# Attention's second pass of scores on 64 rows, two parts of the keys side by side

## The chip, the cores and the metric

The kernel runs on one core of one Trainium2 chip. The metric is the time of the program on the device, in microseconds (us); the page and the views quoted below come from one execution recorded by the hardware profiler.

## The reference

One layer of a streaming encoder on 2048 frames of width 1024. A normalized input is projected to ten groups of columns; one branch is attention in chunks, the other a retention with decay; both are gated, projected, mixed, projected again, added to the input and normalized. The change is in the attention branch, in the first `einsum` of this function:

```python
CHUNK = 64; N_LEFT_CHUNKS = 8; A_HEADS = 8; A_HEAD_DIM = 64

def chunk_band_attention(q, k, v, rel_bias):
    """Each frame attends to its own chunk and the previous N_LEFT_CHUNKS chunks."""
    ...
    def one_sequence(args):
        ...
        s = jnp.einsum('nqhd,nkhd->nhqk', qc, k_band).astype(jnp.float32) * scale + bias[None]
        s = jnp.where(valid[:, None, None, :], s, NEG_INF)
        w = jax.nn.softmax(s, axis=-1).astype(vb.dtype)
        o = jnp.einsum('nhqk,nkhd->nqhd', w, v_band)
        return o.reshape(S, H, d)
```

All in float32, with 8 heads of 64 numbers each. A chunk of 64 queries sees 576 keys.

## The kernel before, in words

**Two parts for each number.** TensorE multiplies in a format (`F32R`) narrower than float32. So each operand is split into a high part, its rounded value, and a low part, what the rounding left. A product of two numbers is then high times high, plus high times low, plus low times high. For keys and queries of 64 numbers this fits the 128 rows of the array: a key tile `kt` holds the high parts of one head's keys on rows 0 to 63 and the low parts on rows 64 to 127, and a query tile `qa` holds both parts of the queries, each of them written twice, on rows 0 to 63 and again on rows 64 to 127. With the high queries as weights, one matmul over 128 rows gives high times high plus high times low: the first pass. With the low queries as weights, a second matmul over the same 128 rows gives low times high (and low times low, which counts for nothing): the second pass.

**Units and slots.** Attention runs in two stages: `heads(0)` for the blocks 0 and 1 of 512 frames, `heads(1)` for the blocks 2 and 3. In a stage, `units` lists (head, block) pairs, 16 of them. The function `slot` issues the work of one slot: for the unit m that is being finished, the transposes of weights and their products with the values (`weighted`), and for the unit after it the scores and the softmax (`soft`). A unit has 12 slots (9 for block 0); `plan` says in which slot which group is handled. In the second stage `soft` for the query tiles t = 0, 1, 2, 3 (128 queries each) of the next unit stands in the slots 2, 6, 8 and 10, in the first stage for block 1 in the slots 1, 3, 5 and 7 of the unit before.

**Fillers.** After each slot `fill(1.0)` runs one step of the dense projections (the gates: matmuls of 512 columns into `ps_g_...`), and `later(n, ...)` puts work on the other engines n steps on. The order on each engine is the order of issue, kept by `keep_in_program_order`; the transfers of attention are on SyncE's queue (SP), which issues them in that order, each one waiting for what it needs.

**`soft`.** For a block b > 0 a query tile sees 640 keys. The scores go to `wide`, three banks of PSUM; since a matmul writes into one bank, the 640 keys are cut into `parts`: 384 and 256 for even t, 256 and 384 for odd t. So a call issues four matmuls: the first pass of both parts, then the second pass of both parts. For block 0 there is one part of 128 to 512 keys and so two matmuls. After that VectorE adds the bias and takes the minimum (`least`), ScalarE takes the exponential, and GpSimd divides.

**Loads.** `load_k` brings a unit's keys, 1024 of them (the block before and the block itself), in slot 6, two units ahead, into one of two buffers. `load_q` brings the queries of two tiles. `load_u` brings the unit's gate into a buffer of the ring `E`, in slot 6; that ring has `E_ATT` = 11 buffers of 128 x 512 numbers and also holds the queries, the values, the transposed weights and the outputs. GpSimd multiplies the unit's output with the gate in `out_`, called by the last group of `weighted`, some five slots into the next unit, and `put` then sends the product off.

Of the kernel before, what the change touches and what calls it, by code (L numbers as in the profile page):

```python
# [11 lines left out]
F32 = mybir.dt.float32  # L12
F32R = mybir.dt.float32r
# [8 lines left out]
P = 128  # L22
# [6 lines left out]
B = 512  # L29
# [23 lines left out]
LO_LAG = 4  # L53
CS = 6
E_PROJ = 19
E_ATT = 11
E_RET = 22
E_MRG = 23
PR_BUFS = 5
# [14 lines left out]
def hybrid_kernel(  # L74
# [30 lines left out]
    def r32(ap):  # L105
        return ap.bitcast(F32)
# [7 lines left out]
    def E(name, dt=F32, shape=(P, 512)):  # L114
        return epool[0].tile(list(shape), dt, tag="e", name=name)
# [4 lines left out]
    def D(name, shape, dt=F32):  # L120
        return dram.tile(list(shape), dt, name=name)
# [31 lines left out]
    pe, act, dve, pool = Ordered(nc.tensor), Sometimes(nc.scalar), Sometimes(nc.vector), Sometimes(nc.gpsimd)  # L153
    dma = Ordered(nc.sync).dma_start
# [19 lines left out]
    kascr = [[D(f"kas_{h}_{b}", [P, B], F32R) for b in range(NB)] for h in range(HEADS)]  # L174
# [70 lines left out]
    def later(n, fn):  # L245

        order[0] += 1
        deferred.append((steps[0] + n, order[0], fn, free[0]))
        deferred.sort(key=lambda e: e[:2])
# [21 lines left out]
    class Chunk:  # L271
# [14 lines left out]
        def half(self, j, c):  # L286
            if self.job.paired[self.c]:

                return self.raw[j].rearrange("p k (i h c) -> p k h i c", i=4, h=2)[:, :, c]
            return self.raw[j][:, :, c * P:(c + 1) * P]  # L290
# [45 lines left out]
    class Strassen(Chunk):  # L336
        tag = ""
# [335 lines left out]
    def step():  # L673
        steps[0] += 1
        while deferred and deferred[0][0] <= steps[0]:
            emit()
        going = next(stream[0], None) is not None
        free[0] = False
        while deferred and not going:
            emit()  # L680
        return going

    def fill(n):
        credit[0] += n
        while credit[0] >= 1.0 and steps[0] < limit[0] and step():
            credit[0] -= 1.0
        credit[0] = min(credit[0], 1.0)
# [722 lines left out]
    def attention(s, sbp, ps_wide):  # L1410
# [3 lines left out]
        kts, vts, qts, bts, uts, oas, prs = {}, {}, {}, {}, {}, {}, {}  # L1414
        units = [(h, b) for h in range(HEADS) for b in (2 * s, 2 * s + 1)]
        wholes = {}

        def load_k(h, b):
            kts[h, b] = sbp.tile([P, 2 * B], F32R, tag="kt", bufs=2, name=f"ka_{h}_{b}")
            for n in range(1 if b == 0 else 0, 2):  # L1420
                dma(r32(kts[h, b][:, n * B:n * B + B]), r32(kascr[h][b - 1 + n]))

        def load_v(h, b):
            vts[h, b] = E(f"va_{h}_{b}", F32R, (P, 4, P))
            dma(r32(vts[h, b]).rearrange("p t c -> p (t c)"), r32(vascr[h][b]))

        def load_vs(h, b):
            if s and b == 2:
                load_v(h, 1)
            load_v(h, b)  # L1430

        def load_q(h, b, un):
            q = E(f"qa_{h}_{b}_{un}", F32R, (P, 2, T))
            rows = qascr[h // 2][b][64 * (h % 2):64 * (h % 2) + 64, un]
            for half in range(2):
                dma(r32(q[64 * half:64 * half + 64]), r32(rows))
            qts[h, b, un] = q

        def load_u(h, b):
            uts[h, b] = E(f"ua_{h}_{b}")[0:64]  # L1440
            dma(uts[h, b], uascr[h // 2][b][64 * (h % 2):64 * (h % 2) + 64])

        def load_bias(h):

            row = escr[h]
            bt = sbp.tile([P, WIN], F32, tag="bt", bufs=2, name=f"bt_{h}")
            if s:
                near = bt[:, 384:640]
                dma(near, bandscr[h])
            else:  # L1450
                near = E(f"near_{h}")[:, 0:256]
                dma(near, bass.AP(tensor=row.tensor, offset=row.offset, ap=[[1, P], [1, 256]]))
            bts[h] = bt, near

        def turn_bias(h):

            bt, near = bts[h]
            bts[h] = bt
            edge = near[:, 0:1] if s else near[:, 255:256]

            def far():
                for n in range(3):
                    act.copy(bt[:, P * n:P * n + P], edge.broadcast_to([P, P]))

            def close():
                if not s:
                    act.copy(bt[:, 384:640], near[:, ::-1])
                    pool.memset(bt[0:64, WIN - 64:WIN], MASK)
                    put(4, bandscr[h], bt[:, 384:640])
                pool.memset(bt[64:128, 0:64], MASK)  # L1470

            later(1, close)
            later(0, far)

        def soft(h, b, t):

            un, a = divmod(t, 2)
            nm = f"{h}_{b}_{t}"
            if b > 0:
                s0, c0 = ((P, 384), (WIN + P, 256))[a]  # L1480
                parts = [(0, c0), (c0, WIN)]
                w, k0 = WIN, t * P
            else:
                s0 = 1024 * a
                w, k0 = (t + 1) * P, B
                parts = [(0, w)]
            sp = wide[:, s0:s0 + w]
            k = kts[h, b]
            q = qts[h, b, un]
            for part in range(2):  # L1490
                for j0, j1 in parts:
                    pe.matmul(
                        sp[:, j0:j1], q[:, part, a * P:(a + 1) * P], k[:, k0 + j0:k0 + j1],
                        start=(part == 0), stop=(part == 1),
                    )
            mn = small.tile([P, 1], F32, tag="mn", name=f"mn_{nm}")
            rsum = small.tile([P, 1], F32, tag="rsum", name=f"rsum_{nm}")
            bt = bts[h]

            def least():  # L1500
                pair, at = (t, 0) if b > 0 else ((0, 0), (1, 0), (1, 2 * P), (0, P))[t]
                if (h, b, pair) not in wholes:
                    wholes[h, b, pair] = sbp.tile([P, WIN], F32, tag="pr", bufs=PR_BUFS, name=f"pr_{nm}")
                prs[h, b, t] = wholes[h, b, pair][:, at:at + w]
                dve.tensor_tensor_reduce(
                    prs[h, b, t], sp, bt[:, WIN - w:WIN], 1.0, 3.0e38, ALU.add, ALU.min, mn,
                )

            def exps():
                pr = prs[h, b, t]  # L1510
                act.activation(pr[:, 0:w], pr[:, 0:w], AF.Exp, bias=mn, scale=-1.0, accum_out=rsum)

            def normed():
                pr = prs[h, b, t]
                dve.reciprocal(rsum, rsum)
                pool.tensor_scalar(pr[:, 0:w], pr[:, 0:w], rsum, 1.0, ALU.mult, ALU.mult)

            later(1, least)
            later(2, exps)
            later(4, normed)  # L1520
# [53 lines left out]
        def slot(m, n, groups, softs):  # L1574

            after = units[m + 1] if m + 1 < len(units) else None
            if n == 0 and after:
                h, b = after
                load_q(h, b, 1)
                if b == 2 * s and h + 1 < HEADS:  # L1580
                    load_bias(h + 1)
                if b == 2 * s + 1 and h + 1 < HEADS:
                    turn_bias(h + 1)
            if n == 6:
                if m + 2 < len(units):
                    load_k(*units[m + 2])
                if m >= 0:
                    load_u(*units[m])
            if n in groups and m >= 0:
                weighted(*units[m], groups[n])  # L1590
            if n in softs and after:
                soft(*after, softs[n])

        load_bias(0)
        load_k(*units[0])
        load_q(*units[0], 0)
        fill(12)
        turn_bias(0)
        fill(2)
        for m in range(-1, len(units)):  # L1600
            length, *plans = plan(units[m][1] if m >= 0 else 2 * s + 1)
            for n in range(length):
                slot(m, n, *plans)
                if n == length - 2 and m + 2 < len(units):
                    load_q(*units[m + 2], 0)
                if n == length - 1 and m + 1 < len(units):
                    load_vs(*units[m + 1])
                fill(ATT_FILL if m >= 0 or n > 1 else 0)
        fill(PV_LAG + 3)

# [257 lines left out]
    for s in range(2):  # L1868
        jobs.append(Job(f"ba{s}", 4, w_stream(w_out_attn, [T * c for c in range(4)], 1), ep_ba(s),
                        kh=1, resident=RYA[s], before=before_ba(s)))  # L1870
# [59 lines left out]
    def heads(s):  # L1930

        st = open_phase(f"att{s}", E_ATT)
        with tc.tile_pool(name=f"sbp{s}", bufs=1, reuse_waits="tile") as sbp:
# [22 lines left out]
    for key in ("b11", "b12", "b21", "b22"):  # L1956
        ch.b[key] = E(f"{key}_p1", shape=(P, 4, P))
        j, h = int(key[1]) - 1, int(key[2]) - 1
# [83 lines left out]
```

## Time and profile before

| | us |
|---|---|
| median of 3 runs | 1908.64 (1907.68 to 1913.85) |
| the profiled execution | 1909.69 |
| its span, first to last instruction | 1907.9 |
| scores of the first stage, first matmul to last | 341.4 to 542.8 |
| scores of the second stage, first matmul to last | 1052.6 to 1296.3 |

How to read the rows that follow: an operation is written as output<-inputs by the names in the program, with partitions x elements. PE is TensorE's matmul, PEld its weight load, DVE VectorE, ACT ScalarE, POOL GpSimd, and SPq the queue of transfers that SyncE issues. `wide` are the scores, `tp` the transposes of the weights, `po` the products with the values, `ps_g_...` the dense filler. Every row has the same line number, since all instructions are issued by one helper; so the names tell them apart. A matmul's duration contains its way through the array; the next matmul starts before that is over, so the distance from start to start is what it costs in a stream. A row of a wait reads: engine and what it was about to do, what it waited for, us in total, times, longest.

### The profile page before, as it was taken

The page shows a single profiled execution, that of the slowest core. Times are in us where ns is not written, and L with a number is a line of the kernel's source. Part 1 is how long each engine was busy: PE and PEld are TensorE (multiplying, and loading weights), DVE is VectorE, ACT ScalarE, POOL GpSimd, SP SyncE. Part 2 cuts the span into 40 slices and gives each one's busy share as a digit, 9 for nine tenths or more (in the row PEclk, how much of TensorE's full clock was granted, in tenths as well). Part 3 has the DMA queues.
Part 4 walks back from the last instruction along what each step waited for, and adds up shares of the span by engine and source line. Part 5 has one row for each costly group of instructions (what it writes and reads, how often), then busy time and mean ns, then how long its engine had stood idle before and what let it go on. Part 6 is the DMA issues. An engine that isn't in the chain of part 4 may idle for free. (4 is left out here: it accounts for less than half of the span.)

```text
span 1907.9 us, 31062 instructions
## 1 busy us (share of the span) xinstructions
PE 1866.9 (98%) x10213; PEld 1604.4 (84%) x10213; DVE 1355.7 (71%) x2456; ACT 933.1 (49%) x1931; POOL 665.3 (35%) x583
## 2 busy tenths in 40 slices
PE   7999999999999999999999999999999999999998
PEld 6899889888888888899889888887888878888886
DVE  6879888677655658889798677765546766767665
ACT  7555554666654455443333666664455321223544
POOL 0102105455645561001105554554564000002775
PEclk9999999999999999999999999999999999999999
DMA  6586976666549987775776656555998999986673
GB/s 197 158 275 200 282 265 213 185 193 185 175 144 278 279 257 258 231 233 195 222 247 202 185 165 180 166 150 155 275 283 265 326 355 345 322 291 227 209 238 127
DMA packets 325553, 435.88 MB, mean 228 GB/s; under 512 B 29880, under 2 KB 191184, under 8 KB 325392
## 3 DMA queue, kind: packets, MB, share of 16 engines
q1 hardware_dynamic: 260096, 368.35, 60.7%
q10 hardware_dynamic: 65296, 65.55, 11.2%
q8 instruction: 81, 1.33, 0.3%
q14 instruction: 80, 0.66, 0.1%
HBM read 288.14 MB, written 145.64 MB: 227 GB/s over the span
## 5 line engine op out<-in xcount | busy, mean ns | idle before, releaser
L143 POOL TENSOR_SCALAR pr<-pr,rsum 128x640 f32<-128x640 f32 (+4 forms) x128 | 100.0, 781 | 197.7 <-DVE rsum L143 130.7
L143 DVE TENSOR_TENSOR ptl<-tp,pth 128x512 fp32r<-128x512 f32 (+1 forms) x168 | 100.3, 597 | 91.7 <-ACT pth L143 77.8
L143 ACT ACTIVATE pr<-pr,mn 128x640 f32<-128x640 f32 (+4 forms) x128 | 97.9, 765 | 123.3 <-DVE mn L143 97.3
L143 PE MATMUL ps_g_x<-r,wh_g 128*128 128x512 f32 x448 | 141.5, 397 | 1.0 <-ACT u_g L143 0.9
L143 PE MATMUL ps_g_z<-r,wh_g 128*128 128x512 f32 x448 | 141.1, 396 | 0.0
L143 POOL TENSOR_TENSOR l_vr<-vrt,h_vr 128x512 fp32r<-128x512 f32 x32 | 47.7, 1492 | 202.4 <-DMA qrs<-l_q 131.6
L143 POOL TENSOR_TENSOR t_out<-raw_out 128x512 f32<-128x512 f32 x7 | 14.1, 2008 | 263.2 <-DVE wl_out L143 263.2
L143 DVE CUSTOM_DVE_ANT_0 pr<-wide,bt 128x640 f32<-128x640 f32 (+4 forms) x128 | 93.7, 732 | 16.5 <-PE wide L143 13.5
L143 ACT CAST pth<-tp 128x512 fp32r<-128x512 f32 (+1 forms) x168 | 85.3, 507 | 38.9 <-PE tp L143 34.2
L143 PE MATMUL wide<-ka,qa 128*128 128x384 f32 (+1 forms) x448 | 94.9, 327 | 2.9 <-DVE mn L143 2.7
L143 DVE TENSOR_TENSOR sm<-sr,dm 128x384 f32<-128x384 f32 x64 | 35.6, 556 | 85.3 <-PE sr L143 33.9
L143 ACT CAST wh_p<-raw_p 128x512 fp32r<-128x512 f32 x111 | 67.9, 618 | 51.0 <-PE ps_p_y L143 18.2
L143 POOL TENSOR_TENSOR sl<-sm,sh 128x384 fp32r<-128x384 f32 x64 | 69.8, 1090 | 64.8 <-ACT sh L143 44.0
L143 PEld LDWEIGHTS tp<-ident,pr 128*128 128x128 f32 x560 | 71.8, 141 | 23.5 <-POOL pr L143 1.0
L143 PEld LDWEIGHTS ps_g_x<-r,wh_g 128*128 128x128 f32 x448 | 79.6, 189 | 13.9 <-ACT u_g L143 2.3
L143 PEld LDWEIGHTS ps_g_z<-r,wh_g 128*128 128x128 f32 x448 | 79.5, 188 | 12.4
L143 PE MATMUL tp<-ident,pr 128*128 128x128 f32 x560 | 89.0, 272 | 0.3
L143 PE MATMUL ps_g_z<-r,wl_g 128*128 128x512 f32 x224 | 88.2, 394 | 0.0
L143 PE MATMUL ps_g_x<-r,wl_g 128*128 128x512 f32 x224 | 88.1, 393 | 0.0
L143 POOL TENSOR_TENSOR wl_g<-t_g,wh_g 128x512 fp32r<-128x512 f32 x56 | 75.5, 1349 | 35.1 <-ACT wh_g L143 33.8
L143 DVE TENSOR_TENSOR wl_p<-raw_p,wh_p 128x512 fp32r<-128x512 f32 x111 | 79.5, 723 | 7.7 <-ACT wh_p L143 5.4
L143 POOL TENSOR_TENSOR t_g<-raw_g,t_g 128x512 f32<-128x512 f32 x56 | 73.8, 1318 | 28.1 <-issue 8.9
(927 smaller groups left out, 6016.7 us busy)
## 6 DMA issues: line engine op xcount, KB each, us to landing
raw_g<-in_w_in_dram ACTq DMA_DIRECT2D x56, 512.0 KB, 4.9
raw_p<-in_w_in_dram ACTq DMA_DIRECT2D x50, 512.0 KB, 5.8
qa<-qas SPq DMA_DIRECT2D x128, 128.0 KB, 3.4
qr<-qrs SPq DMA_DIRECT2D x128, 128.0 KB, 4.8
vr<-vrs SPq DMA_DIRECT2D x64, 256.0 KB, 5.6
ka<-kas SPq DMA_DIRECT2D x56, 256.0 KB, 4.1
va<-vas SPq DMA_DIRECT2D x40, 256.0 KB, 3.4
kds<-kdt_k SPq DMA_DIRECT2D x32, 256.0 KB, 4.8
```

The lines of the kernel that those rows point to most:

```text
L143: return tc.keep_in_program_order(op(*a, **k))
```

## The change

The second pass (low parts of the queries, row 1 of the query tile) is taken over 64 rows only: low queries times the high parts of the keys. One part of the keys is taken from `kt`, rows 0 to 63, as before; the other from a new tile `both`, on whose rows 64 to 127 a copy of the high parts of 512 of the unit's 1024 keys is loaded (`load_again`, two transfers for a unit). The queries' copy on rows 64 to 127 is the weight there. The shorter of the two matmuls is issued first. Where a tile's copy is not yet there (t = 0 of a unit in the second stage), and for block 0, the second pass takes rows 0 to 63 for all parts, one after the other. Rows 0 to 63 of `both` hold the unit's gate, which had a buffer in the ring `E`; the ring has one buffer fewer, and the gate is loaded in slot 7 and not 6.

```diff
-E_ATT = 11
+E_ATT = 10
...
+        both = sbp.tile([P, B], F32, tag="both", name="both")
...
+            if b == 1:
+                load_again(h, b)
+
+        def load_again(h, b):
+            dma(both[64:128, 0:P], r32(kascr[h][b - 1][0:64, 3 * P:]))
+            dma(both[64:128, P:], r32(kascr[h][b][0:64, 0:3 * P]))
...
         def load_u(h, b):
-            uts[h, b] = E(f"ua_{h}_{b}")[0:64]
+            uts[h, b] = both[0:64]
             dma(uts[h, b], uascr[h // 2][b][64 * (h % 2):64 * (h % 2) + 64])
...
-            for part in range(2):
+            qc = slice(a * P, (a + 1) * P)
+
+            def half(n, j0, j1):
+                kh = (both.bitcast(F32R)[64:128, k0 + j0 - 3 * P:k0 + j1 - 3 * P] if n else k[0:64, k0 + j0:k0 + j1])
+                pe.matmul(sp[:, j0:j1], q[64 * n:64 * n + 64, 1, qc], kh, start=False, stop=True)
+
+            for j0, j1 in parts:
+                pe.matmul(sp[:, j0:j1], q[:, 0, qc], k[:, k0 + j0:k0 + j1], start=True, stop=False)
+            if b > 0 and (t or not s):
+                for n, (j0, j1) in sorted(enumerate(parts if t < 3 else parts[::-1]), key=lambda x: x[1][1] - x[1][0]):
+                    half(n, j0, j1)
+            else:
                 for j0, j1 in parts:
-                    pe.matmul(
-                        sp[:, j0:j1], q[:, part, a * P:(a + 1) * P], k[:, k0 + j0:k0 + j1],
-                        start=(part == 0), stop=(part == 1),
-                    )
+                    half(0, j0, j1)
...
                 if m + 2 < len(units):
                     load_k(*units[m + 2])
-                if m >= 0:
-                    load_u(*units[m])
+            if n == 7 and m >= 0:
+                load_u(*units[m])
...
         load_k(*units[0])
+        if s:
+            load_again(*units[0])
...
                     load_vs(*units[m + 1])
+                    if s and m + 2 < len(units):
+                        load_again(*units[m + 2])
```

## The prediction

> **What bounds the kernel now.** I read the page first, then the windows of the two attention stages, then what TensorE waited for there, and last single instructions of one slot.
>
> ```profile
> span 1907.9 us, 31062 instructions
> PE 1866.9 (98%) x10213; PEld 1604.4 (84%) x10213; DVE 1355.7 (71%) x2456; ACT 933.1 (49%) x1931; POOL 665.3 (35%) x583
> ```
>
> TensorE is busy for 98% of the span. An average says little about one stage, so here are the two stretches in which scores are computed (columns: length, busy time and instructions of each engine, granted clock, DMA share, GB/s), and the two longest waits of TensorE in each, first for the first stretch, then for the second:
>
> ```profile
> 341.10:522.00 180.90, 177.85 (x968) 149.94 (x967) 129.27 (x312) 118.79 (x279) 102.58 (x118) 1.00 0.62 183
> 1080.00:1296.50 216.50, 214.64 (x1212) 183.33 (x1210) 151.72 (x335) 134.82 (x295) 112.30 (x111) 1.00 0.55 167
> ```
> ```profile
> PEld wide L143 <- DVE mn L143: 4.8, 7, 1.5
> PE wide L143 <- DVE mn L143: 2.3, 3, 1.1
> ```
> ```profile
> PEld po L143 <- DVE oa L143: 5.3, 9, 0.9
> PE po L143 <- DVE oa L143: 1.9, 6, 0.4
> ```
>
> TensorE idles for 180.90 - 177.85 = 3.05 us in the first and 216.50 - 214.64 = 1.86 us in the second. VectorE is at 71% and 70%, ScalarE and GpSimd lower, the DMA engines at 0.62 and 0.55. So TensorE's own stream sets the pace in both, and time that really leaves that stream leaves the kernel, less what waits grow by.
>
> **What one call of soft costs now.** One call, quoted instruction by instruction (start in us, duration; a row with x2 or x3 is a merged run whose start is the first one's):
>
> ```profile
> 1103.79 0.19 PEld L143 LDWEIGHTS wide<-ka,qa 128*128 128x128 f32 x1
> 1104.07 0.31 PEld L143 LDWEIGHTS wide<-ka,qa 128*128 128x128 f32 x2
> 1104.19 0.19 PEld L143 LDWEIGHTS wide<-ka,qa 128*128 128x128 f32 x1
> 1104.37 0.19 PEld L143 LDWEIGHTS po<-pth,va 128*128 128x128 f32 x1
> 1104.07 0.57 PE L143 MATMUL wide<-ka,qa 128*128 128x256 f32 x3
> 1104.19 0.45 PE L143 MATMUL wide<-ka,qa 128*128 128x384 f32 x2
> 1104.37 0.28 PE L143 MATMUL wide<-ka,qa 128*128 128x256 f32 x1
> 1104.48 0.40 PE L143 MATMUL po<-pth,va 128*128 128x512 f32 x1
> 1104.48 0.19 PEld L143 LDWEIGHTS po<-ptl,va 128*128 128x128 f32 x1
> ```
>
> Call the four matmuls of a call W1 to W4. First pass: W1 (384 columns), W2 (256, starts 1104.07). Second pass: W3 (384, 1104.19), W4 (256, 1104.37); then po at 1104.48. So 384 columns take 0.18 us and 256 take 0.11 to 0.12, and the second pass costs 1104.48 - 1104.19 = 0.29 us. Two habits of the weight loads matter below. Each load starts at the moment the matmul ahead of it starts (1104.07, 1104.19, 1104.37, 1104.48 stand on both sides), so it lies under that matmul. And a load needs about 0.11 us before its matmul can run: W4 starts 0.18 after its own load at 1104.19, but po's, loaded at 1104.37, starts 0.11 later.
>
> **The change part by part.** How many calls it touches:
>
> ```profile
> L143 PE MATMUL wide<-ka,qa x448: 221/336/481, 341.4 to 1296.3; 128*128 128x384 f32 x74, 128*128 128x256 f32 x60, 128*128 128x128 f32 x8, 128*128 128x512 f32 x8
> L143 DVE CUSTOM_DVE_ANT_0 pr<-wide,bt x128: 273/815/826, 342.0 to 1297.3; 128x640 f32<-128x640 f32 x96, 128x128 f32<-128x128 f32 x8, 128x512 f32<-128x512 f32 x8, 128x256 f32<-128x256 f32 x8
> ```
>
> There are 128 calls, 96 of them 640 keys wide. By the condition (b > 0, and t > 0 or s = 0) the halves lie side by side in 8 x 4 = 32 calls of the first stage and 16 x 3 = 48 of the second: 80. The other 48 (16 with 640 keys, 32 with one part) get 64-row matmuls one after the other. The count of matmuls and loads stays at 448; only their rows and order change.
>
> *Removed.* If the 256-column half runs beside the 384-column half, the second pass takes 0.18 instead of 0.29 us: 0.11 x 80 = 8.8 us. In the 48 others the number of columns stays, so I take 0; the bounds are those of the switch below.
>
> *Weight loads.* A load of fewer rows isn't shorter in this trace: the one with 8 rows took 0.17 us, as long as the loads around it.
>
> ```profile
> 9.03 0.17 PEld L143 LDWEIGHTS gains<-ident,gains 8*128 8x128 f32 x1 [9.03 <-issue]
> 9.76 0.18 PEld L143 LDWEIGHTS pa<-ident,xa 128*128 128x128 f32 x1 [0.55 <-DVE xa L143]
> ```
>
> So the loads of W3 and W4 still want 0.11 us each. They go to different rows. Bounds: if both are ready when W2 ends, nothing is lost; if the load of W4 begins only when W3 starts, as every load does in the rows above, W4 starts 0.11 behind W3 and the pass takes 0.11 + 0.18 = 0.29, all of the 8.8 us. No load here meets others of other rows, so this is open; I take the first end, because the second depends on the array refusing a load for rows that no pending matmul uses.
>
> The Trainium skill, "TensorE: Matmul & The Clock Gate", section "Part 3: Packing small matmuls", says for this case that matmuls in different row groups start about 4 ns apart and that loads of another row group are pulled ahead. By that the gain would be 80 x (0.11 - 0.004) = 8.5 us. No run here shows it yet.
>
> *Switching between 128 and 64 rows,* twice in each of 128 calls, 256 times. The nearest row is a switch to another shape of weights, 32 columns, in retention:
>
> ```profile
> 655.30 0.39 PE L143 MATMUL ps_g_w<-r,wl_g 128*128 128x512 f32 x1
> 655.31 0.11 PEld L143 LDWEIGHTS ssq<-o2h,ohr 128*32 128x32 f32 x1
> 655.53 0.28 PE L143 MATMUL ssq<-o2h,ohr 128*32 128x256 f32 x1
> 655.65 0.28 PE L143 MATMUL ssq<-o2l,ohr 128*32 128x256 f32 x1
> 655.88 0.28 PE L143 MATMUL ssq<-o2l,ohr 128*32 128x256 f32 x1
> 655.88 0.19 PEld L143 LDWEIGHTS o<-sh,vr 128*128 128x128 f32 x1
> 656.00 0.28 PE L143 MATMUL o<-sh,vr 128*128 128x256 f32 x1
> ```
>
> Going in, 512 columns take 0.23 us (655.30 to 655.53), and coming out, 256 take 0.12 (655.88 to 656.00): the price is zero, one end. The other end is a full emptying of the array: a matmul of 512 columns lasts 0.39 us but lets the next one in after 0.23, so its tail is 0.16 us, and 256 x 0.16 = 41 us. A gain at a switch is excluded, since no matmul can start before the one ahead has taken in its columns. I take 0, the nearest row, though it narrows columns and not rows.
>
> *Moved and added on the DMA queue.* load_again adds two transfers in 24 units (heads and blocks with b > 0), 48 on SP's queue; load_u moves one slot later and into a single buffer.
>
> ```profile
> 1129.33 0.45 SPq L143 DMA_DIRECT2D ua<-uas  x1
> 1131.39 1.29 POOL L143 TENSOR_TENSOR oa<-oa,ua 64x512 f32<-64x512 f32 x1
> 1132.70 0.47 SPq L143 DMA_DIRECT2D oas<-oa  x1
> 1133.98 1.08 SPq L143 DMA_DIRECT2D qa<-qas  x2
> ```
>
> The new u may be written only after GpSimd's product for the unit before has read the old one, here at 1131.39 + 1.29 = 1132.68. Behind the waiting load_u on SP stands oas, which waits for that same product today, so the queue loses one issue of 0.45 us, and the next qa (1133.98) has 0.8 us to spare. load_again waits for the last scores of the unit ahead; behind it stand the next unit's query rows for its third and fourth call, needed about eight slots on.
>
> ```profile
> 1101.04 0.83 PE L143 MATMUL wide<-ka,qa 128*128 128x256 f32 x4
> 1103.81 0.83 PE L143 MATMUL wide<-ka,qa 128*128 128x384 f32 x4
> ka<-kas SPq DMA_DIRECT2D x56, 256.0 KB, 4.1
> ```
>
> These two calls are two slots apart, 2.77 us, so a slot is 1.39 us. The copy goes out at slot 11 and is used at slot 6 of the next unit: 7 x 1.39 = 9.7 us, against 4.1 us to landing for a whole 256 KB key block. I cost it at 0; it is covered by 5.6 us, and past that every microsecond of lateness costs one in 16 units. The bounds are 0 and 16 us (one microsecond late in each). One E buffer fewer: ua held one of the 11 from slot 6 to slot 17 of a 12-slot unit, so the others keep about ten; 0, and below nothing only by noise.
>
> *Sum.* -8.8 us on TensorE. Part of it comes back as waits for VectorE, whose reading of wide already stops TensorE for 4.8 + 2.3 us in the first stage; if calls come 4% sooner (0.11 of 2.77 us) I let those and the 5.3 + 1.9 us on po grow by a total of 1 us, an estimate. Net -7.8 us. The profiled execution took 1909.7 us (span 1907.9), so 1901.9 against it; it is 1.1 us over the median of the three runs, 1908.6, against which the forecast is **1900.8 us**.
>
> **The rivals.**
> *The loads space the halves.* W4's load starts with W3, as in all rows above. Then small first and large second give 0.11 + 0.18 = 0.29, nothing gained: 1908.6. If both loads are pulled ahead under W2, one behind the other, W4 can start 0.22 after W2: where W2 has 256 columns the call ends at 0.22 + 0.18 = 0.40 instead of 0.12 + 0.29 = 0.41, and where it has 384 at 0.40 instead of 0.18 + 0.29 = 0.47. With 32 and 48 such calls that is 0.3 + 3.4 = 3.7 us, 1904.9. For it: load starts tied to matmul starts. Against: those were all loads of the same rows. That the halves do not run together at all ends at the same 1908.6.
>
> *The array empties at each switch.* All 128 calls pay twice, also the 48 that gain nothing. At the full tail: 1908.6 + 41 - 8.8 = 1940.8. It decides from 7.8 / 256 = 0.03 us a switch on; above that the kernel is slower. For it: the tail of 0.16 us exists, and no row shows a change in the number of rows within a busy stream. Against: the free switch at ssq. The Trainium skill, "TensorEngine Tiling (Array Packing)", section "Key Properties", speaks for this rival: changing the tiling mode, not just the tile, drains TensorE. It gives no time; whether the ssq rows are such a mode the profile does not say.
>
> *The copy of the keys is late.* 16 units of the second stage, a microsecond each: 1908.6 - 7.8 + 16 = 1916.8, only if SP is held back over 5.6 us.
>
> **How the numbers follow.** Side by side as forecast 0.42; loads space the halves (or the halves run in turn) 0.26; emptying at the switches 0.27; late copy 0.05. About 0.3% (5.7 us) is what a measurement of this kernel can tell from no change. Faster by more: the forecast nearly whole, 0.41. Within: the spaced halves, a weak forecast, and a switch of about 0.03 us (0.04): 0.31. Slower: the rest, 0.28. The range goes from 1898 (all 8.8 us and some noise) to 1941 (the full tail); the likeliest case's own range is 1898 to 1903.
>
> **What would show it.** In the changed trace, W3 and W4 should start within a few hundredths of a microsecond, and the matmul after them 0.18 us later; W4 0.11 behind W3 speaks for the loads; W3 more than 0.18 (0.12) behind W2, or a longer gap to po, for the switch, and then the 48 unpaired calls show it alone. Waits of TensorE for a DMA of both would show the late copy; GpSimd's product on u and SP's oas should keep their places. The prediction is wrong if TensorE's busy time in the two stretches does not fall by some 8 us.

## The result, and the profile after

The changed kernel is slower: 1938.6 us against 1910.0 us for the kernel before in the same comparison, a ratio of 1.0151 with a 95% interval from 1.0127 to 1.0175. The forecast was 1900.8 us and faster; the time came out beside the rival that empties the array at each switch (1940.8 us). The page of the changed kernel's profiled execution begins:

```profile
span 1940.4 us, 31141 instructions
PE 1904.1 (98%) x10213; PEld 1599.9 (82%) x10213; DVE 1354.4 (70%) x2456; ACT 937.5 (48%) x1931; POOL 666.5 (34%) x583
```

As many matmuls and loads as before, 37 us more of busy TensorE, and the busy time of VectorE, ScalarE and GpSimd as it was within a few microseconds. So the time was added in TensorE's own stream, where the prediction had hoped to take it away. The same view as before of the two stretches, each now from its first matmul of scores to its last:

```profile
339.50:561.80 222.30, 219.21 (x1075) 167.77 (x1073) 144.00 (x348) 132.77 (x307) 110.50 (x127) 0.98 0.56 166
1069.60:1326.70 257.10, 257.10 (x1353) 201.70 (x1351) 168.69 (x379) 154.89 (x333) 124.58 (x124) 1.00 0.55 167
```

Before, these two lasted 542.8 - 341.4 = 201.4 and 1296.3 - 1052.6 = 243.7 us: 20.9 and 13.4 us more, 34.3 us together. The spans differ by 32.5 us, so everything was added in these two stretches, and the rest of the kernel came out 1.8 us shorter.

A few of the 20.9 us belong to this one execution, which took 1942.2 us, 3.6 more than the median. The granted clock of the first stretch was 0.98, before it was 1.00. It was low around the end of one wait of TensorE, for a transfer of queries (`qa`); the second row is the window view of the 6.8 us behind that wait, with the clock at 0.53:

```profile
481.81 1.49 PE L143 MATMUL wide<-ka,qa 128*128 128x512 f32 x2 [2.42 <-DMA qa<-qas]
481.80:488.60 6.80, 6.79 (x17) 4.79 (x18) 1.02 (x4) 1.40 (x3) 1.62 (x2) 0.53 0.35 115
```

Beside the wait of 2.4 us, the low clock cost some 6.8 x 0.47 = 3.2 us there, an estimate. Where the wait comes from is taken up with the copies below.

One paired call of the changed kernel (odd t, so W1 has 256 keys and W2 384; then the two halves, W3 with 256 and W4 with 384), instruction by instruction, in the columns of the prediction, with an idle time and what is said to have ended it in brackets:

```profile
1126.98 0.54 PE L143 MATMUL wide<-ka,qa 128*128 128x256 f32 x2
1127.07 0.19 PEld L143 LDWEIGHTS wide<-ka,qa 128*128 128x128 f32 x1
1127.19 0.34 PE L143 MATMUL wide<-ka,qa 128*128 128x384 f32 x1
1127.45 0.18 PEld L143 LDWEIGHTS wide<-both,qa 64*128 64x128 f32 x1 [0.19 <-issue]
1127.45 0.38 PE L143 MATMUL wide<-both,qa 64*128 64x256 f32 x1
1127.46 0.18 PEld L143 LDWEIGHTS wide<-ka,qa 64*128 64x128 f32 x1
1127.46 0.44 PE L143 MATMUL wide<-ka,qa 64*128 64x384 f32 x1
1127.82 0.19 PEld L143 LDWEIGHTS po<-pth,va 128*128 128x128 f32 x1 [0.18 <-ACT pth L143]
1127.83 0.44 PE L143 MATMUL po<-pth,va 128*128 128x384 f32 x1
1127.93 0.19 PEld L143 LDWEIGHTS po<-ptl,va 128*128 128x128 f32 x1
1128.11 0.34 PE L143 MATMUL po<-ptl,va 128*128 128x384 f32 x1
```

Two things are to be seen. The halves do run side by side: their loads start 0.01 us apart, and so do the matmuls (unrounded, 3 to 4 ns in each of the 80 pairs). And at both borders of the 64-row part the habit that the prediction read off the kernel before is broken: the load no longer starts with the matmul ahead of it. The load of W3 should have started at 1127.19 with W2; it starts at 1127.45, 0.08 us before W2's recorded end (1127.19 + 0.34 = 1127.53). In the same way the load for po starts at 1127.82, 0.08 before W4's end (1127.46 + 0.44 = 1127.90). No weight is being loaded for 0.19 and 0.18 us meanwhile; the releaser named in the second bracket, `ACT pth`, is only the last semaphore that the load waited for, and the first bracket names none. After a load that isn't hidden the matmul must still wait 0.11 us. Its row doesn't say so at once, since it starts with the load, at 1127.83; but it lasts 0.44 us, 0.10 more than the next one with as many columns (0.34), and the load after it, which elsewhere starts with the matmul ahead, starts at 1127.93. So a switch does not let the next matmul begin when the last one has taken in its columns, but some 0.03 us after the last one's recorded end: its tail of 0.16 us and 0.03 more, 0.19 us. (This profile models the ends of matmuls and doesn't measure them. The prices below are taken from starts.)

### The profile page after: what moved, and what is told of

It is laid out like the page before. It is cut to its first block, busy times and chain, and to the rows that moved or that the text cites. A ratio compares the mean times of both kernels' runs of the same rounds, so it can differ in the third digit from the quotient of the medians.

```text
span 1940.4 us, 31141 instructions
## 1 busy us (share of the span) xinstructions
PE 1904.1 (98%) x10213; PEld 1599.9 (82%) x10213; DVE 1354.4 (70%) x2456; ACT 937.5 (48%) x1931; POOL 666.5 (34%) x583
## 4 chain that ended last, share of the span: by engine, by line
PE 84%; DMA 8%; DVE 3%; ACT 2%; issue 1%; SPq 1%; POOL 0%; ACTq 0%; DVEq 0%; POOLq 0%
PE ps_g_x L143 7%; PE ps_g_z L143 7%; PE ps_p_z L143 7%; PE ps_p_x L143 7%; PE po L143 4%; PE wide L143 4%; PE ps_g_v L143 4%; PE ps_g_y L143 3%; PE ps_p_y L143 3%; PE ps_g_w L143 3%; PE ps_p_v L143 3%; PE ps_p_w L143 3%; PE tp L143 3%; PE ps_out_z L143 2%; PE ps_out_x L143 2%; PE o L143 2%
## 5 line engine op out<-in xcount | busy, mean ns | idle before, releaser
L143 PE MATMUL wide<-ka,qa 128*128 128x384 f32 (+5 forms) x368 | 108.9, 369 | 2.8 <-DMA qa<-qas 2.4
```

The source lines that it names most:

```text
L143: return tc.keep_in_program_order(op(*a, **k))
```

## The experiments

The theory after this reading is a price for each switch between 128 and 64 rows. The rival is that what came along with it (two copies of keys for a unit, one ring buffer fewer, the gate loaded later into a single buffer) holds TensorE back. All times are medians, the ratios are to the kernel before in the same comparison.

**The switch alone.** In the kernel before:

```diff
             for part in range(2):
                 for j0, j1 in parts:
+                    r = 64 if part else P
                     pe.matmul(
-                        sp[:, j0:j1], q[:, part, a * P:(a + 1) * P], k[:, k0 + j0:k0 + j1],
+                        sp[:, j0:j1], q[0:r, part, a * P:(a + 1) * P], k[0:r, k0 + j0:k0 + j1],
```

> The kernel before, with only the second pass changed: rows 0 to 63 in all 128 calls, one part after the other; no copy of the keys, ring, loads and slots as before. Theory (the switch): each change between 128 and 64 rows empties TensorE (0.10 us) and leaves the next weight load unhidden (0.11 us), 0.42 us a call, 54 us in all, of which waits that TensorE had anyway may take up to a quarter: 1950 to 1964 us. Rival (the copies, the smaller ring and the later gate hold TensorE back): none of that is in it, so the time of before, 1910 us.

Measured: 1949.0 us, ratio 1.0214 (1.0195 to 1.0233), 40.7 us more than the 1908.4 us of before. The switch alone costs all that the change costs and more; with the halves side by side (1938.6) it is 10.5 us less. The time is a microsecond short of the expected range, since less came through than I had allowed for. The price of a call is read best from calls of the same kind, 256 then 384 keys, with the products of 384 columns behind them, first in the kernel before, then in this one, from the first matmul of scores to the second of po:

```profile
1106.59 0.83 PE L143 MATMUL wide<-ka,qa 128*128 128x256 f32 x4
1107.43 0.34 PE L143 MATMUL po<-ptl,va 128*128 128x384 f32 x1
```
```profile
1113.44 1.03 PE L143 MATMUL wide<-ka,qa 128*128 128x256 f32 x4
1113.91 0.29 PEld L143 LDWEIGHTS wide<-ka,qa 64*128 64x128 f32 x2 [0.19 <-issue]
1114.67 0.34 PE L143 MATMUL po<-ptl,va 128*128 128x384 f32 x1
```

Before 1107.43 - 1106.59 = 0.84, here 1114.67 - 1113.44 = 1.23, in the changed kernel above 1128.11 - 1126.98 = 1.13. Taken in this way for all 128 calls, each against the same call of the kernel before, the growth has a median of 0.39 us here, and in the changed kernel of 0.39 for the 48 unpaired and 0.27 for the 80 paired calls. So two switches cost 0.39 us a call; the pair gives back 0.10 to 0.12 of it.

**The copies alone.** In the changed kernel, with all that it loads and holds kept:

```diff
-            for j0, j1 in parts:
-                pe.matmul(sp[:, j0:j1], q[:, 0, qc], k[:, k0 + j0:k0 + j1], start=True, stop=False)
...
+            for part in range(2):
+                for j0, j1 in parts:
+                    pe.matmul(sp[:, j0:j1], q[:, part, qc], k[:, k0 + j0:k0 + j1], start=(part == 0), stop=(part == 1))
```

> The changed kernel with every second pass on 128 rows as before; the two copies per unit are still loaded (into rows that nothing reads), the ring has 10 buffers, the gate is in the new tile and loaded in slot 7. Theory (the switch): 1910 us, within 0.3%. Rival (copies, ring, gate): most of the 29 us stays, 1930 to 1939 us.

Measured: 1911.4 us, ratio 1.0015 (1.0000 to 1.0030). As the cause of the 29 us the rival falls: the copies, the ring and the queue cost between nothing and 0.3%.

They aren't wholly free. In the first stretch TensorE waits for queries in all five kernels that have the copies, for 1.1 to 2.4 us in total, and in none of the others. In the changed kernel the queue ahead of that wait looks like this:

```profile
469.57 1.75 POOL L143 TENSOR_TENSOR oa<-oa,both 64x512 f32<-64x512 f32 x1
471.35 0.45 SPq L143 DMA_DIRECT2D both<-uas  x1
471.90 1.18 SPq L143 DMA_DIRECT2D qa<-qas  x2
474.45 1.08 SPq L143 DMA_DIRECT2D qa<-qas  x2
```

The gate has only one buffer now, and GpSimd's product reads it until 469.57 + 1.75 = 471.32. The next gate's load waits for that, with the queries behind it, and the later queries leave 3.13 us after the product. In the kernel before, the gate and the first queries left ahead of the same product (at 457.32 and 461.10; it ended at 464.65), and the later queries 1.16 us after it, at 465.81. So in the changed kernel these leave some 2 us later, and TensorE, which had no wait there, now waits 2.4 us.

**Only the pairs.** In the changed kernel, for calls that have no partner:

```diff
-                    half(0, j0, j1)
+                    pe.matmul(sp[:, j0:j1], q[:, 1, qc], k[:, k0 + j0:k0 + j1], start=False, stop=True)
```

> The changed kernel with the 48 calls that have no partner back on 128 rows in the second pass; the 80 paired calls as changed. Theory (the switch): 48 x 0.42 = 20 us less, of which a quarter may be waits again: 1918 to 1924 us, still slower than before, since a pair saves less than its two switches cost. Rival (copies, ring, gate): 1938 us as changed.

Measured: 1927.4 us, ratio 1.0100 (1.0082 to 1.0118). The direction is the theory's, and pairs alone are slower than before; but the 48 calls gave back 11.2 us and not 14 to 20. In the waits of TensorE's weight loads over the whole span a part of the difference can be seen. First the kernel before, then this one:

```profile
PEld po L143 <- DVE oa L143: 6.5, 11, 0.9
PEld wide L143 <- DVE mn L143: 6.5, 12, 1.5
```
```profile
PEld po L143 <- DVE oa L143: 3.6, 9, 0.6
PEld wide L143 <- DVE mn L143: 3.3, 6, 1.6
```

In e1_rows64 0.5 and 1.1 us are left of them. With TensorE slowed, VectorE is mostly in time and these waits go; where switches are taken away, they come back in part. How much of the switches' price was taken up between the calls is added up under "The sum" below.

**Other numbers of rows.** The same edit as in e1_rows64 with 96 and with 32 in place of 64.

> The kernel before with the second pass on rows 0 to 95 in all 128 calls (half of the low-times-low products left out), nothing else. If the switch is one between 128 rows and one half of the array, as I think: 1910 us, loads stay hidden. Rival (any change in the number of rows empties the array): as the same kernel with 64 rows, 1950 to 1964 us.

> The kernel before with the second pass on rows 0 to 31, so half of each low-times-high product and all low-times-low ones are left out. If any block of fewer than 128 rows is a state of its own with the same price at its borders: as e1_rows64, 1945 to 1952 us. If the price grows with how far the rows shrink: above 1955 us.

Measured: 96 rows 1910.1 us, ratio 1.0006 (0.9993 to 1.0019); 32 rows 1945.4 us, ratio 1.0213 (1.0178 to 1.0247). A change from 128 to 96 rows costs nothing that can be measured, one to 64 or to 32 the same. With 96 rows the loads are where they were, hidden and in step:

```profile
1101.21 0.60 PEld L143 LDWEIGHTS wide<-ka,qa 128*128 128x128 f32 x4
1101.80 0.19 PEld L143 LDWEIGHTS po<-pth,va 128*128 128x128 f32 x1
1101.92 0.19 PEld L143 LDWEIGHTS po<-ptl,va 128*128 128x128 f32 x1
```

(The row of four names the shape of the first one of them.) So the price isn't paid for any change in the number of rows, and it doesn't grow from 64 rows to 32. A reading that fits is that a pass over 96 rows still takes the array whole and one over 64 or 32 a block of it; that is argued. Where between 64 and 96 the price sets in, no run shows.

**Twice the switches.** The kernel of e1_rows64 with the two loops exchanged:

```diff
-            for part in range(2):
-                for j0, j1 in parts:
+            for j0, j1 in parts:
+                for part in range(2):
                     r = 64 if part else P
```

> The kernel before with the second pass on rows 0 to 63 as in e1_rows64, but each part's two passes stand together, so the 96 calls of 640 keys change between 128 and 64 rows four times and not twice; same matmuls, same columns. Theory (a price for each switch, 0.39 us for a pair of switches as e1_rows64's trace shows): 96 x 0.39 = 37 us more than e1_rows64's 1949, so 1980 to 1990 us. Rival (64-row matmuls or their loads are slow in themselves, or a price for each call): 1949 us.

Measured: 1983.5 us, ratio 1.0404 (1.0379 to 1.0429), 34.4 us over e1_rows64: 34.4 / 96 = 0.36 us for each further pair of switches. In the trace the median call of 640 keys is 0.78 us longer than before, twice the 0.39 of e1_rows64. These are the same matmuls over the same columns, in another order. So the price belongs to the borders and not to the 64-row matmuls, and here, where few waits for VectorE were left to give way, it comes through nearly whole.

**The order of the passes, and of the halves.** In the changed kernel, the low queries first, and in another one the longer half first:

```diff
-            for j0, j1 in parts:
-                pe.matmul(sp[:, j0:j1], q[:, 0, qc], k[:, k0 + j0:k0 + j1], start=True, stop=False)
             if b > 0 and (t or not s):
...
+            for j0, j1 in parts:
+                pe.matmul(sp[:, j0:j1], q[:, 0, qc], k[:, k0 + j0:k0 + j1], start=False, stop=True)
```

> The changed kernel with the pass of the low queries first and the pass over 128 rows second. The price of going in is emptying (0.10 us) and a load that is not hidden (0.11 us); after the transposes the first load of a call is unhidden by 0.09 us anyway, and a transpose of 128 columns is through sooner. Theory: some 0.06 us a call is saved, 128 x 0.06 = 8 us: 1927 to 1934 us. Rival (a flat price for a switch, whatever stands around it): 1938 us.

```diff
-                for n, (j0, j1) in sorted(enumerate(parts if t < 3 else parts[::-1]), key=lambda x: x[1][1] - x[1][0]):
+                for n, (j0, j1) in sorted(enumerate(parts if t < 3 else parts[::-1]), key=lambda x: x[1][0] - x[1][1]):
```

> The changed kernel with the longer half of a pair issued first. Theory (both weight loads of a pair run at the same time, as the changed trace shows them starting 0.01 us apart): order does not matter, 1938 us. Rival of the prediction (the second half's load waits for the first half's start): 0.06 us a pair less, about 1934 us.

Measured: low first 1938.6 us, ratio 1.0170 (1.0146 to 1.0194); longer half first 1940.6 us, ratio 1.0175 (1.0148 to 1.0201). The second agrees with loads that run at the same time. The first is a miss: I had expected 1927 to 1934 us. The rows of low first say why, an unpaired call with the transposes ahead of it:

```profile
1126.88 0.49 PE L143 MATMUL tp<-ident,pr 128*128 128x128 f32 x3
1127.30 0.29 PEld L143 LDWEIGHTS wide<-ka,qa 64*128 64x128 f32 x2 [0.17 <-issue]
1128.63 0.39 PE L143 MATMUL ps_g_z<-r,wl_g 128*128 128x512 f32 x1
```

The transposes' recorded end is 1126.88 + 0.49 = 1127.37, and the load starts 0.07 us before it. A transpose takes in only 128 columns, but it lasts 0.27 us (the three start 0.11 us apart and take 0.49 together), about as long as a matmul of 256 columns (0.28 in the prediction's rows), so little is gained by putting the border behind it. From the transposes to the third filler matmul the call takes 1128.63 - 1126.88 = 1.75 us; an unpaired call of the kernel with the longer half first, in the old order of passes, takes 1129.06 - 1127.30 = 1.76:

```profile
1127.30 0.49 PE L143 MATMUL tp<-ident,pr 128*128 128x128 f32 x3
1129.06 0.40 PE L143 MATMUL ps_g_z<-r,wl_g 128*128 128x512 f32 x1
```

At a switch the next load follows the recorded end of the last matmul, not its intake.

## Why the prediction was wrong, point by point

**What bounds the kernel: right.** TensorE's stream sets the pace of both stretches; what was added to it came out in the time.

**The pair's gain: right.** 8.8 us were forecast (0.11 us in 80 calls). The rows give 0.10 to 0.12 us a call, 8 to 10 us; the changed kernel is 10.5 us below e1_rows64 (the ratios, 1.0151 and 1.0214, differ by 0.0063 with an uncertainty of about 0.003, 6 to 18 us).

**The weight loads of a pair: right.** I took the end at which nothing is lost, and the loads start 0.01 us apart. By the rule of the Trainium skill, "TensorE: Matmul & The Clock Gate", section "Part 3: Packing small matmuls", a load of other rows is pulled ahead and the matmuls start about 4 ns apart; the trace agrees within the blocks of 64 (3 to 4 ns in each of the 80 pairs), but a load is not pulled ahead over the border into them. The prediction's remark that no matmul can start before the one ahead has taken in its columns doesn't hold for the two halves. The rival of spaced halves falls with this row and with e8_large_first.

**The copies, the ring and the queue: nearly right, at 0.** e2_copies_only is within 0.3% of before. The prediction read the queue off one place in the second stage, where the next queries had 0.8 us to spare. In the first stage the single gate buffer made queries late, by 2.4 us in the changed kernel's trace.

**The switch: this is the step that failed.** The prediction put a price on it between 0 and 0.16 us and took 0, "the nearest row, though it narrows columns and not rows". The runs showed 0.39 us for a pair of switches, 0.19 each, even a little above the upper end: the bound had the tail of the matmul, but left out that the next load isn't hidden any more. The row at ssq says nothing of a change in rows; it was near only in that something else narrowed. Its own caveat should have kept the value between the ends, and at the 0.03 us from which the rival decides a price anywhere in the upper four fifths of 0 to 0.16 made the kernel slower. The rule that the prediction quoted from the Trainium skill, "TensorEngine Tiling (Array Packing)", section "Key Properties", that changing the tiling mode drains TensorE, agrees with what the traces show for 128 rows against 64: the next load waits until 0.07 us before the recorded end of the last matmul, and the new matmul runs 0.03 us after it.

**The sum.** From the rows: 48 unpaired calls x 0.39 + 80 paired calls x 0.29 = 18.7 + 23.2 = 41.9 us on TensorE. Measured are 28.6 us. For e1_rows64 it is 128 x 0.39 = 49.9 against 40.7. So 13 and 9 us are missing, and the traces show where. Added up from the starts of the matmuls, the 128 calls of e1_rows64, each from its first matmul of scores to the second matmul behind the call, grew by 48.6 us, about what the rows say. What lies between the calls of the two stages shrank by 10.3 us, 6.6 of them at 26 matmuls whose weight load had waited over 0.15 us before, mostly for VectorE (the 6.5 + 6.5 us shown above), and does so no more. In the changed kernel the calls grew by 40.4 us, and what lies between them shrank by 5.3 us in the second stage; in the first stage the late queries and the low clock took back nearly all that was saved. The prediction had the waits for VectorE grow by 1 us; since TensorE became slower, they shrank.

The measured time lies within the prediction's range of 1898 to 1941 us, since that reached as far as the rival. The forecast itself, 7.8 us less, had the wrong direction. That the rival's time came out so near (1940.8 and 1938.6) is partly luck: 0.16 us a switch was too little, and no waits were taken off.

## What to carry to other kernels

Two small matmuls side by side on half the rows each save about what the shorter one takes, here 0.10 us, but going from the whole array into blocks of 64 rows and back costs 0.39 us: at these sizes a single pair between 128-row matmuls loses. By these two numbers about four pairs would have to stand together without a switch to break even, an estimate that no run has tried. Here a pass over 96 of the 128 rows took as long as one over all of them (ratio 1.0006), so leaving rows out gained nothing, and going down to 64 or 32 cost 2%. Where the trace has no row for an operation, a row that resembles it in one respect only is a bound and not a value.

## What the runs showed of the hardware that was not expected

A switch between 128 rows and 64 holds back not only the next matmul but its weight load: at each of the 256 borders of the changed kernel, and at each of those of e1_rows64, it starts 0.07 us before the recorded end of the last matmul (0.07 to 0.08 by the rounded rows above), and the new matmul runs 0.11 us after it. Blocks of 32 rows pay what blocks of 64 pay (ratios 1.0213 and 1.0214), and 96 rows pay nothing (1.0006). The weight loads of the two halves, 0.11 us apart where one follows the other, run at the same time on different halves of the rows.

The granted clock can fall to about half within a kernel that is busy otherwise: 0.53 for the 6.8 us behind one wait of 2.4 us. The shorter waits for queries in the other kernels with the copies, at most 1.8 us each, had a clock of 1.00 behind them. What made it fall, no run shows.
